# First attention and even mixer of a two-block model: stores on other queues, a modulation part moved, every fourth convolution tap on TensorE

## The chip, the cores and the metric

The kernel runs on one core of one Trainium2 chip. The metric is the device time of one execution in microseconds (us), lower is better.

## The reference

Two blocks run one after the other. The parts that this case is about, cut down:

```python
def first_block(x, c, ctx, c_ctx, ada_w, ...):
    for i in range(2):
        shift, scale, gate = split(silu(c) @ ada_w[i] + ada_b[i], 3)
        h_lat = rms_norm(x_lat, norm_w[i]) * (1 + scale) + shift       # 1024 tokens, width 1024
        ...                                                            # i == 0: also 256 context tokens
        y = attn_mixer(h_lat, h_ctx, ...) if i % 2 == 0 else hyena_mixer(h_lat, ...)
        x_lat = x_lat + gate * y
    return rms_norm(x_lat, final_norm_w)

def attn_project(h, ...):
    q_a, k_a, v_a, c_q, c_kv, k_pe, gate = split_cols(h @ w_in, ATTN_SPLITS)
    # 8 grouped heads of 64 on 2 key heads: q_a, k_a are normalised per head and rotated (rope)
    # 8 latent heads: q_m = norm(c_q) @ w_uq (64 + 32 rotated), k_m, v_m = norm(c_kv) @ w_ukv, k_pe shared
    ...
def mix(...):
    o = concat(softmax(q_a k_a) v_a, softmax(q_m k_m) v_m)             # keys: 256 context + 1024 tokens
    return (o * silu(gate)) @ w_out

def even_mixer(h, in_w, dw_w, dw_b, ...):                              # in second_block
    a_val, a_gate, q, k, v = split(h @ in_w, ...)
    u = causal_dwconv(a_val * sigmoid(a_gate), dw_w, dw_b)             # 512 channels, 31 taps each
    u = silu(layer_norm(u, ln_g, ln_b))
    o = stick_breaking_attention(rms_norm(heads(q)), rms_norm(heads(k)), heads(v))
    return concat(u, o) @ out_w
```

## The kernel before

Activations lie channels on partitions (128) and tokens along the free axis. Products at full precision are made from three matmuls: `split` (L100, L104) cuts an operand into a rounded high part (`...h`, ScalarE) and a rest (`...l`, VectorE), and `mm3` (L108 to L110) multiplies high by high, high by low and low by high. A framework of tiles and pools places the semaphores: a tile of a pool with n buffers waits until the one n tiles earlier is no longer read. It also sets each engine's order, from the order in which the code is written.

**A modulation row** is a product of a weight row block with the silu of `c`. `mods` (L226) loads 128x1024 weights at L228 on SyncE's queue and multiplies and sums them on VectorE at L236. It is a generator, one row block per `step`; `finish_aside` runs it to the end. Of the first block's 48 row blocks, 16 are needed before the first projection, and 32 (16 to 47) only later.

**First attention, projections** (`_a_project`, L338). `proj` (L348) multiplies the weights of one column block with 512 (or 256 context) tokens. Keys, then grouped queries, latent ranks and gates follow; each result goes through a norm per head (L405), `rope` (L388 to L395: a shuffle and three element-wise operations, one of them on GpSimd in 10 of 14 cases) and `store` (L411), which splits it into `sth` and `stl`, two buffers each, and writes the two to memory by SyncE's queue (L424). The destination holds two heads of 64 rows, so that its outermost size is 2 (4 for the rotated parts of latent queries). Values (`vstore`, L426) and gates (`gate`, L477, L480) are stored by the same queue, and weights (L328), rope tables and the 32 modulation blocks are loaded by it, the latter two buffers deep, one per projection. A second generator `both` makes the keys and values of the latent heads (22 steps) and their queries (12, L537); from the fifth projection on each loop turn takes one step of it. At the end `a_load` (L588) loads the first pair of heads on GpSimd's queue (qa, qb, ka, kb, v), and the steps left follow.

**First attention, attention** (`_a_attend`, L623). For 8 pairs of heads and 2 halves of the queries, 10 key blocks each: scores (L686), Exp on ScalarE (L123), the sum of weights on VectorE (`acc`, L735) and weighted values (L692). Meanwhile the next group's maximum is estimated: `guess` (L666) writes scores of 128 queries into `s`, a PSUM tile with a single buffer, and VectorE reduces it (L669). `finish` (L697 to L709) divides by the sum, with a tile `z`, one buffer. `moe_clear` (L1760) sets a tile of the same tag `z` to zero and stores it thirteen times to `m_y`, which the experts use much later; it is called in the second group.

**Even mixer** (`ev_mixer`, L1425). `conv(n)` runs four times on 128 channels: it makes value and gate by `proj_tile` (PSUM tag `pj`, three buffers), and `u` with 30 zeros ahead. Of the 31 taps the last starts `acc` on ScalarE, 20 of the rest go to VectorE (L1474, one fused multiply-add over 1024 tokens each), and every third to ScalarE, which multiplies (L1468), and GpSimd, which adds (L1470) into `accp`; L1476 adds the two sums. A generator again: `queries_keys` takes steps of it (its norm is L297 and L155 to L157), so that taps stand between the projections.

```python
                nc.vector.stream_shuffle(sh, x, mask)
                eng.tensor_tensor(out=x, in0=x, in1=ropes[0][:m, 0, t0:t0 + n], op=ALU.mult)
...
                if j % 3 == 2:
                    t = accp if first else cp.tile([P, T], F32, name="ct", tag="ct")
                    nc.scalar.mul(t, src, wcol)
```

Of the kernel before, what the change touches and what calls it, by code (L numbers as in the profile page):

```python
# [18 lines left out]
P = 128  # L19
# [69 lines left out]
class Kern:  # L89
# [175 lines left out]
    def phase_a(self, first, mod, M):  # L265

        tc = self.tc
        with tc.tile_pool(name="a_dram", bufs=1, space=DRAM) as dr:
# [5 lines left out]
            self._a_project(*first, S, mod)  # L274
            o_pool = tc.alloc_tile_pool(name="a_o", bufs=1, side="right")
            o = o_pool.tile([P, KT, T], F32, name="attn_o")
            self._a_attend(first[0], o, S, M)
# [60 lines left out]
    def _a_project(self, A, lat_ab, ctx_ab, S, mod):  # L338
        tc, nc, a = self.tc, self.nc, self.a
        PARTS = ((0, 512), (512, 512), (T, TC))  # L340
        if True:
# [6 lines left out]
            def proj(wc, c0, m, part, xh=hh, xl=hl, nk=KT):  # L348
                t0, n = part
                ps = pp.tile([P, 512], F32, name="mm", tag="mm")[:m, :n]  # L350
                if nk == KT:
                    self.step()
                for k in range(nk):
                    self.mm3(ps, wc[0][:, k, c0:c0 + m], wc[1][:, k, c0:c0 + m], xh[:, k, t0:t0 + n],
                             xl[:, k, t0:t0 + n], k == 0, k == nk - 1)
                return ps
# [21 lines left out]
            self.aside = self.mods(tp, a["ada_wT"].rearrange("l r d -> (l r) d"), ("c",), (mod,), 16, 48, 2)  # L378
# [9 lines left out]
            def rope(x, part, mask, eng=nc.gpsimd):  # L388
# [4 lines left out]
                eng.tensor_tensor(out=x, in0=x, in1=ropes[0][:m, 0, t0:t0 + n], op=ALU.mult)  # L393
# [17 lines left out]
            def store(x, dst, off, step, hs, d, pitch, part, rep=1):  # L411

                t0, n = part
                hl_ = [tp.tile([P, 512], F32R, name="st" + q, tag="st" + q)[:x.shape[0], :n] for q in "hl"]
                self.split(hl_[0], hl_[1], x)
                for i, t in enumerate(hl_):
# [7 lines left out]
                    nc.sync.dma_start(ap_of(dst, i * off * pitch + t0, dims), src.bitcast(F32))  # L424

            def vstore(ps, dst, b):  # L426
                t = tp.tile([P, 512], F32, name="vs", tag="vhl")[:, :ps.shape[1]]
                nc.scalar.copy(t, ps)
                nc.sync.dma_start(dst[:, b], t)
# [47 lines left out]
            def gate(m, pt, ps):  # L477
                g = work(P, 512)
                self.act(g, ps, AF.Silu)
                nc.sync.dma_start(S["gate"][m, :, pt[0]:pt[0] + 512], g)  # L480

            def key_rope(pt, ps):
# [4 lines left out]
                if pt[0] < T:  # L487
                    rope(kp, pt, swap8, nc.vector)
# [48 lines left out]
            def latent_queries():  # L537
                self.finish_aside()
                msc = 96.0 ** -0.5
                for m in range(6):  # L540
                    if m in (0, 4):
                        c = (0, 512) if m == 0 else (512, 256)
                        k = 2 * c[1]
                        w = A.wp.tile([P, 1024], F32, name="wraw", tag="wraw")[:, :k]
                        nc.sync.dma_start(w, a["w_uq"][:, 2 * c[0]:2 * c[0] + k])
                        wuq = [tp.tile([P, 1024], F32R, name="wq", tag="modw")[:, :k] for _ in "hl"]
                        self.split(*wuq, w)
                        wuq = [t.rearrange("p (k c) -> p k c", k=2) for t in wuq]
                    for pt in PARTS[:2]:
# [5 lines left out]
                        else:  # L555
                            rope(x, pt, swap8, nc.vector)
# [8 lines left out]
            for n, (ps, post) in enumerate(projections()):  # L565
# [3 lines left out]
                if n >= 4:  # L569
                    next(beside, None)  # L570
            last()
            self.finish_aside()
# [50 lines left out]
    def _a_attend(self, A, o, S, M):  # L623
# [7 lines left out]
        with tc.tile_pool(name="at_o", bufs=2) as op, tc.tile_pool(name="at_s", bufs=1, space=PSUM) as sp, \  # L631
                tc.tile_pool(name="at_t", bufs=3, space=PSUM) as tp, \
                tc.tile_pool(name="at_p", bufs=1, space=PSUM) as pp:
            st, gates = {}, {}

# [84 lines left out]
            for i, (hp, g) in enumerate(todo):  # L720
                if i == 1:
# [5 lines left out]
                for kb in range(NK):  # L727
# [23 lines left out]
            while pend:  # L751
                pend.pop(0)()
        for p in (A.ip[1], ptp, wp, A.ip[0]):
# [676 lines left out]
    def ev_mixer(self, F, x_pool, work, h, S):  # L1430
# [12 lines left out]
        def conv(n):  # L1443
# [17 lines left out]
            accp = cp.tile([P, T], F32, name="accp", tag="accp", bufs=1)  # L1461
            first = True
            for j in range(30):
                src = u[:, j:j + T]
                wcol = self.vec("ev_dw_w", j * 4 + n)
                if j % 3 == 2:
                    t = accp if first else cp.tile([P, T], F32, name="ct", tag="ct")
                    nc.scalar.mul(t, src, wcol)  # L1468
                    if not first:
                        nc.gpsimd.tensor_tensor(out=accp, in0=accp, in1=t, op=ALU.add)  # L1470
                    first = False
                    yield
                else:
                    nc.vector.scalar_tensor_tensor(out=acc, in0=src, scalar=wcol, in1=acc, op0=ALU.mult,  # L1474
                                                   op1=ALU.add)
            nc.gpsimd.tensor_tensor(out=acc, in0=acc, in1=accp, op=ALU.add)  # L1476
# [1080 lines left out]
```

## Time and profile before

| | |
|---|---|
| median of 3 runs | 4418.02 us (4414.76 to 4423.42) |
| the profiled execution's own time | 4418.37 us |
| its span, first to last instruction | 4416.6 us |
| mean granted TensorE clock | 0.91 of full speed |
| TensorE busy | 3641.1 us (82%) |
| VectorE busy | 2981.7 us (68%) |
| ScalarE busy | 1810.4 us (41%) |
| GpSimd busy | 1149.5 us (26%) |

In the profile PE is TensorE, PEld its weight loads, DVE VectorE, ACT ScalarE, POOL GpSimd and SP SyncE; a q behind the name is the engine's queue. L12 is line 12 of the kernel. An operation reads out<-in. The granted clock is TensorE's, as a share of full speed. DMA is the mean busy share of the core's 16 DMA engines. Shares over the whole span are averages over stages with different limits, so the stages are read one by one: the projections stand from 345 to 805 us, the attention from 822 to 1336, the convolutions of the even mixer from 2336 to 2590.

### The profile page before, as it was taken

Reading aid. Unit: us, or ns where it says so; the run is one execution under the profiler, and the core shown is the slowest. Engines: PE = TensorE matmul, PEld = TensorE weight load, DVE = VectorE, ACT = ScalarE, POOL = GpSimd, SP = SyncE. Lnnn points to the kernel's source line nnn. Section 1 sums busy time; section 2 is a strip of 40 time slices with the busy share of each in tenths; the row PEclk is TensorE's granted clock in tenths of the full one; section 3 lists DMA queues with packets and bytes.
Section 4 is the critical chain, followed back from the end, with each engine's and each line's share of the span. In section 5 each row is a group of like instructions: output and inputs, shape, how many; then the busy total and the mean of one; then the engine's idle time right before and its main releaser. Section 6 shows DMA issues by size and latency. Waiting matters only on the chain. (4 is left out here: it accounts for less than half of the span.)

```text
span 4416.6 us, 45389 instructions
## 1 busy us (share of the span) xinstructions
PE 3641.1 (82%) x16768; PEld 2823.9 (64%) x16768; DVE 2981.7 (68%) x3254; ACT 1810.4 (41%) x2470; POOL 1149.5 (26%) x640
## 2 busy tenths in 40 slices
PE   5786576599998999867787757788999788879997
PEld 4774454345556877756665646667888576767885
DVE  7995341577665676799678969755666576556664
ACT  4552231244443212111244435545556454436663
POOL 4630000011110001488304345331111133411112
PEclk9897788799999999988898879889999899989998
DMA  4553343422304786333321133227787511258876
GB/s 160 169 168 105 116 157 104 146 65 60 71 21 167 265 292 205 115 126 132 129 100 63 58 97 92 82 81 264 287 283 284 184 46 39 96 181 312 289 289 215
DMA packets 213107, 675.07 MB, mean 153 GB/s; under 512 B 40757, under 2 KB 66793, under 8 KB 177810
## 3 DMA queue, kind: packets, MB, share of 16 engines
q1 hardware_dynamic: 160738, 548.86, 35.7%
q0 software_dynamic: 44656, 97.06, 7.7%
q10 hardware_dynamic: 7488, 26.22, 1.5%
q8 instruction: 133, 2.18, 0.2%
q14 instruction: 92, 0.75, 0.1%
HBM read 538.04 MB, written 133.94 MB: 152 GB/s over the span
## 5 line engine op out<-in xcount | busy, mean ns | idle before, releaser
L104 DVE TENSOR_TENSOR wl<-wraw,wh 128x1024 fp32r<-128x1024 f32 (+1 forms) x212 | 330.0, 1565 | 223.1 <-ACT wh L100 206.9
L100 ACT CAST wh<-wraw 128x1024 fp32r<-128x1024 f32 (+1 forms) x212 | 276.0, 1312 | 448.8 <-DMA wraw<-in_ex_w_dram 151.1
L108 PE MATMUL pj<-hh,wh 128*128 128x512 f32 x1024 | 406.3, 397 | 19.4 <-ACT hh L881 7.6
L108 PE MATMUL mm<-hh,wh 128*128 128x512 f32 (+3 forms) x832 | 344.9, 415 | 82.6 <-ACT wh L100 22.3
L109 PE MATMUL pj<-hl,wh 128*128 128x512 f32 x1024 | 411.2, 402 | 0.0
L110 PE MATMUL pj<-hh,wl 128*128 128x512 f32 x1024 | 405.1, 396 | 0.7 <-DVE wl L104 0.7
L110 PE MATMUL mm<-hh,wl 128*128 128x512 f32 (+3 forms) x832 | 335.8, 405 | 7.4 <-DVE wl L104 7.3
L109 PE MATMUL mm<-hl,wh 128*128 128x512 f32 (+3 forms) x832 | 338.2, 406 | 1.0 <-POOL hl L104 0.8
L123 ACT ACTIVATE pt<-st 128x512 f32<-128x512 f32 x320 | 181.6, 598 | 225.0 <-PE st L686 211.0
L108 PEld LDWEIGHTS mm<-hh,wh 128*128 128x128 f32 (+1 forms) x832 | 165.5, 199 | 136.0 <-ACT wh L100 14.9
L669 DVE TENSOR_REDUCE mx<-s 128x1 f32<-128x1280 f32 x124 | 184.4, 1487 | 97.5 <-PE s L666 97.0
L236 DVE SCALAR_TENSOR_TENSOR modw<-modw,c 128x1024 f32<-128x1024 f32 x128 | 161.2, 1273 | 123.3 <-DMA modw<-in_ada_wT_dram 69.7
L108 PEld LDWEIGHTS pj<-hh,wh 128*128 128x128 f32 x1024 | 196.5, 192 | 67.1 <-ACT hh L881 10.0
L109 PEld LDWEIGHTS pj<-hl,wh 128*128 128x128 f32 x1024 | 196.8, 192 | 45.6 <-issue 4.3
L110 PEld LDWEIGHTS pj<-hh,wl 128*128 128x128 f32 x1024 | 196.2, 192 | 46.5 <-issue 4.3
L104 DVE TENSOR_TENSOR l<-raw,h 128x1024 fp32r<-128x1024 f32 x128 | 166.9, 1335 | 64.9 <-ACT h L100 62.7
L692 PE MATMUL ps_o<-pt,v 128*64 128x512 f32 x640 | 201.6, 609 | 0.0
L1326 PE MATMUL py<-c_g,ph 128*128 128x256 f32 x512 | 134.5, 423 | 79.6 <-DVE ph L1205 79.6
L110 PEld LDWEIGHTS mm<-hh,wl 128*128 128x128 f32 (+1 forms) x832 | 163.8, 197 | 47.7 <-DVE wl L104 10.2
L109 PEld LDWEIGHTS mm<-hl,wh 128*128 128x128 f32 (+1 forms) x832 | 165.1, 198 | 39.8 <-DVE hl L882 1.9
L2206 POOL DMA_INDIRECT xg<-m_h,idx x50 | 65.0, 1300 | 466.1 <-PE xt L2120 420.7
L735 DVE TENSOR_TENSOR acc<-acc,pt 128x1024 f32<-128x1024 f32 x128 | 158.8, 1241 | 21.1 <-ACT pt L123 18.4
(601 smaller groups left out, 9943.0 us busy)
## 6 DMA issues: line engine op xcount, KB each, us to landing
wraw<-in_ex_w_dram SPq DMA_DIRECT2D x128, 1024.0 KB
raw<-in_ex_w_dram SPq DMA_DIRECT2D x64, 1024.0 KB
modw<-in_mod_wT_dram SPq DMA_DIRECT2D x96, 512.0 KB
modw<-in_ada_wT_dram SPq DMA_DIRECT2D x48, 512.0 KB
m_y<-ys ACTq DMA_DIRECT2D x48, 512.0 KB
ks<-kt SPq DMA_DIRECT2D x64, 256.0 KB
wraw<-in_w_hy_in_dram SPq DMA_DIRECT2D x16, 1024.0 KB
kk<-ks SPq DMA_DIRECT2D x28, 512.0 KB
```

Of the source, the lines that this page charges most:

```text
L100: nc.scalar.copy(hi, src)
L104: e.tensor_tensor(out=lo, in0=src, in1=hi.bitcast(F32), op=ALU.subtract)
L108: nc.tensor.matmul(ps, wh, xh, start=first, stop=False)
L109: nc.tensor.matmul(ps, wh, xl, start=False, stop=False)
L110: nc.tensor.matmul(ps, wl, xh, start=False, stop=last)
L123: ins = act.activation(out, in_, func, **kw).ins
L236: nc.vector.scalar_tensor_tensor(out=junk, in0=w, scalar=1.0, in1=c, op0=ALU.mult, op1=ALU.mult, accum_out=o[:, j:j + 1])
L669: nc.vector.tensor_reduce(out=mx[:, j:j + 1], in_=s[:, :TK] if own else m3, op=ALU.max, axis=AX.X, negate=True)
L692: nc.tensor.matmul(ps_o[e * 64:(e + 1) * 64], st[2 * hp + e]["v"][:, kb], pt[:, e], start=kb == 0, stop=kb == NK - 1)
L735: nc.vector.tensor_tensor(out=acc, in0=acc, in1=pt, op=ALU.add)
L1326: nc.tensor.matmul(py[:, j], d["ph"][:, r, cs], g[:, m, r], start=k == 0, stop=k == 3)
L2206: self.nc.gpsimd.indirect_dma_start(out=out, out_offset=None, in_=src, in_offset=bass.IndirectOffsetOnAxis(ap=ix, axis=0))
```

## The change

Stores of `_a_project`: four buffers instead of two for `sth`, `stl` and the values; high parts, values and gates go out on ScalarE's queue, low parts on GpSimd's. SyncE's queue keeps the loads. `rope` multiplies on VectorE in all cases. The 32 modulation blocks leave `_a_project`; `_a_attend` makes them, in a pool with two buffers, one after the third and one after the seventh key block of each group from the second on, the rest at the end. The second generator starts with the eleventh projection instead of the fifth, so six of its steps are left for the time of the first pair's loads; its weights come by the same buffers as the others. `moe_clear` is called in the fourth group instead of the second. In the even mixer taps 3, 7, ... 27 (seven of 30) become matmuls: ScalarE multiplies the identity with the tap's column (`dg`, 128x128), TensorE multiplies `dg` with the shifted `u` at full precision into `side`, a PSUM tile of tag `pj`, and VectorE adds `side` at the end; the other 23 taps are VectorE's.

```diff
@@ _a_project(self, A, lat_ab, ctx_ab, S): without mod
             def proj(wc, c0, m, part, xh=hh, xl=hl, nk=KT):
...
-                if nk == KT:
-                    self.step()
...
-            self.aside = self.mods(tp, a["ada_wT"].rearrange("l r d -> (l r) d"), ("c",), (mod,), 16, 48, 2)
...
-            def rope(x, part, mask, eng=nc.gpsimd):
+            def rope(x, part, mask):
...
-                eng.tensor_tensor(out=x, in0=x, in1=ropes[0][:m, 0, t0:t0 + n], op=ALU.mult)
+                nc.vector.tensor_tensor(out=x, in0=x, in1=ropes[0][:m, 0, t0:t0 + n], op=ALU.mult)
@@ store, vstore, gate
-                hl_ = [tp.tile([P, 512], F32R, name="st" + q, tag="st" + q)[:x.shape[0], :n] for q in "hl"]
+                hl_ = [tp.tile([P, 512], F32R, name="st" + q, tag="st" + q, bufs=4)[:x.shape[0], :n] for q in "hl"]
...
-                    nc.sync.dma_start(ap_of(dst, i * off * pitch + t0, dims), src.bitcast(F32))
+                    (nc.gpsimd if i else nc.scalar).dma_start(ap_of(dst, i * off * pitch + t0, dims), src.bitcast(F32))
...
-                t = tp.tile([P, 512], F32, name="vs", tag="vhl")[:, :ps.shape[1]]
+                t = tp.tile([P, 512], F32, name="vs", tag="vhl", bufs=4)[:, :ps.shape[1]]
                 nc.scalar.copy(t, ps)
-                nc.sync.dma_start(dst[:, b], t)
+                nc.scalar.dma_start(dst[:, b], t)
...
-                nc.sync.dma_start(S["gate"][m, :, pt[0]:pt[0] + 512], g)
+                nc.scalar.dma_start(S["gate"][m, :, pt[0]:pt[0] + 512], g)
@@ latent_queries and the loop
-                self.finish_aside()
...
-                        w = A.wp.tile([P, 1024], F32, name="wraw", tag="wraw")[:, :k]
-                        nc.sync.dma_start(w, a["w_uq"][:, 2 * c[0]:2 * c[0] + k])
-                        wuq = [tp.tile([P, 1024], F32R, name="wq", tag="modw")[:, :k] for _ in "hl"]
-                        self.split(*wuq, w)
-                        wuq = [t.rearrange("p (k c) -> p k c", k=2) for t in wuq]
+                        wuq = self.a_wload(A, a["w_uq"][:, 2 * c[0]:2 * c[0] + k], 2, c[1])
...
-                if n >= 4:
+                if n >= 10:
                     next(beside, None)
             last()
-            self.finish_aside()
@@ _a_attend(self, A, o, S, M, mod)
+            self.aside = self.mods(op, self.a["ada_wT"].rearrange("l r d -> (l r) d"), ("c",), (mod,), 16, 48, 2)
...
-                if i == 1:
+                if i == 3:
                     self.moe_clear(op, M)
...
                         pend.append(functools.partial(finish, hp, g, ps_o, acc))
+                    if i and kb % 4 == 2:
+                        self.step()
...
+            self.finish_aside()
@@ ev_mixer, conv
-            accp = cp.tile([P, T], F32, name="accp", tag="accp", bufs=1)
-            first = True
+
+            side = F.pp.tile([P, T], F32, name="side", tag="pj")
             for j in range(30):
-                src = u[:, j:j + T]
                 wcol = self.vec("ev_dw_w", j * 4 + n)
-                if j % 3 == 2:
-                    t = accp if first else cp.tile([P, T], F32, name="ct", tag="ct")
-                    nc.scalar.mul(t, src, wcol)
-                    if not first:
-                        nc.gpsimd.tensor_tensor(out=accp, in0=accp, in1=t, op=ALU.add)
-                    first = False
+                if j % 4 == 3:
+                    dg = cp.tile([P, P], F32, name="dg", tag="dg", bufs=3)
+                    nc.scalar.mul(dg, self.ident, wcol)
+                    for t in (0, 512):
+                        nc.tensor.matmul(side[:, t:t + 512], dg, u[:, j + t:j + t + 512], start=j == 3, stop=j == 27)
                     yield
                 else:
...
-            nc.gpsimd.tensor_tensor(out=acc, in0=acc, in1=accp, op=ALU.add)
+            nc.vector.tensor_tensor(out=acc, in0=acc, in1=side, op=ALU.add)
```

SyncE's queue in the projections, near the first key stores. Before (`modw` is a modulation block, `wraw` weights, `s_k` and `s_km` the keys):

```order
L228 DMA modw<-in_ada_wT_dram 128x1024 x5
L328 DMA wraw<-in_w_attn_in_dram 128x1024
L424 DMA s_k<-sth 2x64x512
L424 DMA s_km<-sth 2x64x512
L228 DMA modw<-in_ada_wT_dram 128x1024
L424 DMA s_k<-stl 2x64x512
L424 DMA s_km<-stl 2x64x512
```

The same queue now, from the first rope table to the end of the projections and beyond:

```order
L381 DMA ropes<-in_ropes_dram 128x2048
L512 DMA wraw<-in_w_ukv_dram 128x512
L328 DMA wraw<-in_w_attn_in_dram 128x1024 x6
L512 DMA wraw<-in_w_ukv_dram 128x512
L328 DMA wraw<-in_w_attn_in_dram 128x1024 x3
L328 DMA wraw<-in_w_attn_in_dram 128x256
```

Stores and modulation blocks are gone from between the weights. ScalarE in the middle of the projections now (`wk` is a gate or query in work, `mm` a projection's PSUM tile, `s_q` the queries):

```order
L477 DMA s_gate<-wk 128x512
L100 CAST sth<-wk 128x512
L100 CAST sth<-mm 128x512
L421 DMA s_q<-sth 2x64x512
L421 DMA s_km<-sth 2x64x512
L100 CAST sth<-mm 128x512
L287 ACTIVATE sqa<-mm 128x512
```

Each store stands in ScalarE's own order, between its casts and activations. VectorE in the attention, second group, now (`mx` is the guess, `m_l_129` the sums of the modulation):

```order
L661 TENSOR_REDUCE mx<-s 128x1
L236 SCALAR_TENSOR_TENSOR modw,m_l_129<-modw,c 128x1024
L661 TENSOR_REDUCE mx<-s 128x1
L699 SCALAR_TENSOR_TENSOR z<-sm,y 128x512
L727 TENSOR_TENSOR acc<-acc,pt 128x1024
```

Before, a guess and a sum took turns there, and nothing else stood between them but the two operations of `finish`. TensorE in a convolution of the even mixer now (`pj` is a projection, `blk_70` the norm's block matrix):

```order
L108 MATMUL pj<-hh,wh 128x512
L109 MATMUL pj<-hl,wh 128x512
L110 MATMUL pj<-hh,wl 128x512
L1464 MATMUL side<-u,dg 128x512 x4
L297 MATMUL mm<-sqa,blk_70 128x512
L1464 MATMUL side<-u,dg 128x512 x4
L108 MATMUL pj<-hh,wh 128x512
```

Before, the projection's matmuls ran on from one side of L297 to the other, with nothing but it between them.

## Rows read from the trace of the kernel before

**Rows 1.** Stretches by engine; columns: from:to, length, busy time of each engine, clock, DMA share, GB/s

```profile
core 0: us, PE busy (x) PEld busy (x) DVE busy (x) ACT busy (x) POOL busy (x), PEclk, DMA share, GB/s
345.00:805.00 460.00, 262.35 (x999) 194.11 (x997) 164.56 (x268) 115.02 (x182) 21.69 (x17) 0.77 0.37 118
...
822.00:1336.00 514.00, 502.76 (x1982) 264.80 (x1980) 366.34 (x300) 227.28 (x399) 78.60 (x61) 0.99 0.27 71
2336.00:2407.00 71.00, 56.11 (x219) 43.01 (x218) 60.56 (x44) 28.75 (x33) 30.42 (x10) 0.88 0.17 63
2407.00:2473.00 66.00, 47.07 (x177) 35.53 (x176) 60.55 (x44) 29.21 (x33) 30.68 (x10) 0.82 0.21 75
2473.00:2539.00 66.00, 52.01 (x228) 40.85 (x227) 60.87 (x44) 29.77 (x34) 30.71 (x10) 0.87 0.12 45
2539.00:2590.00 51.00, 35.99 (x261) 34.76 (x259) 47.14 (x34) 15.61 (x23) 33.17 (x12) 0.90 0.21 63
```

**Rows 2.** Timeline of SyncE's queue, projections; columns: start, us, instruction

```profile
376.52 0.50 SPq L424 DMA_DIRECT2D s_k<-stl  x1
377.12 5.48 SPq L424 DMA_DIRECT2D s_km<-stl  x1
...
411.86 2.63 SPq L424 DMA_DIRECT2D s_k<-stl  x1
```

**Rows 3.** Stretches, while only key stores are under way

```profile
383.00:402.00 19.00, 6.86 (x20) 5.02 (x21) 4.06 (x7) 1.93 (x3) 0.00 (x0) 0.56 0.13 51
```

**Rows 4.** DMA issues, 345 to 822 us; count, KB each, us to landing

```profile
modw<-in_ada_wT_dram SPq DMA_DIRECT2D x31, 512.0 KB
...
s_qm<-sth SPq DMA_DIRECT2D x12, 256.0 KB
...
s_km<-sth SPq DMA_DIRECT2D x9, 256.0 KB
...
s_q<-sth SPq DMA_DIRECT2D x8, 256.0 KB
...
ka<-s_k POOLq DMA_DIRECT2D x1, 640.0 KB, 26.4
```

**Rows 5.** Waits, 345 to 822 us: total, times, longest

```profile
DVE stl L104 <- DMA s_qm<-stl: 39.6, 5, 11.5
...
PE mm L297 <- ACT sqa L287: 32.7, 6, 11.5
...
PE mm L108 <- ACT wq L100: 18.4, 1, 18.4
...
PE mm L297 <- DVE sqa L291: 14.6, 1, 14.6
```

**Rows 6.** Stretches, while three loads of GpSimd's queue are under way

```profile
2622.00:2626.00 4.00, 0.00 (x0) 0.00 (x0) 0.00 (x0) 0.00 (x0) 0.00 (x0) 0.50 0.43 156
```

**Rows 7.** Modulation's group by line; wait for the scores; ScalarE's timeline; a stretch

```profile
L236 DVE SCALAR_TENSOR_TENSOR modw<-modw,c 128x1024 f32<-128x1024 f32 x32 | 40.0, 1251 | 69.7 <-DMA modw<-in_ada_wT_dram 69.7
...
DVE mx L669 <- PE s L666: 94.3, 58, 4.7
...
866.55 0.60 ACT L123 ACTIVATE z<-sm 128x512 f32<-128x512 f32 x1 [9.55 <-DMA m_y<-z]
...
862.00:866.00 4.00, 0.00 (x0) 0.00 (x0) 0.00 (x0) 0.00 (x0) 0.00 (x0) 0.73 0.12 50
```

**Rows 8.** Even mixer: taps by line and by duration; TensorE's timeline; a wait

```profile
L1474 DVE SCALAR_TENSOR_TENSOR o<-u,vecs,o 128x1024 f32<-128x1024 f32 x80 | 165.0, 2063 | 6.4 <-ACT o L1458 5.2
...
L1474 DVE SCALAR_TENSOR_TENSOR o<-u,vecs,o x80: 1268/1284/3355, 2336.3 to 2583.6; 128x1024 f32<-128x1024 f32 x80
...
2455.89 0.39 PE L108 MATMUL pj<-hh,wh 128*128 128x512 f32 x1
2456.12 1.02 PE L297 MATMUL mm<-sqa,blk 128*128 128x512 f32 x2
...
2457.21 0.39 PE L110 MATMUL pj<-hh,wl 128*128 128x512 f32 x1
...
PE mm L297 <- DVE o L1474: 28.8, 3, 9.9
```

More of the change, by code (lines that the diff above doesn't have):

```diff
@@ L273, in phase_a @@
             S["gate"] = dr.tile([KT, P, T], F32, name="s_gate")
-            self._a_project(*first, S, mod)
+            self._a_project(*first, S)
             o_pool = tc.alloc_tile_pool(name="a_o", bufs=1, side="right")
             o = o_pool.tile([P, KT, T], F32, name="attn_o")
-            self._a_attend(first[0], o, S, M)
+            self._a_attend(first[0], o, S, M, mod)
         return o, o_pool
@@ L336, in a_wchunk, with _a_project @@
         return self.a_wload(A, self.a["w_attn_in"][:, A.off - KT * c:A.off], KT, c)
-    def _a_project(self, A, lat_ab, ctx_ab, S, mod):
+    def _a_project(self, A, lat_ab, ctx_ab, S):
         tc, nc, a = self.tc, self.nc, self.a
@@ L487, in key_rope @@
                 if pt[0] < T:
-                    rope(kp, pt, swap8, nc.vector)
+                    rope(kp, pt, swap8)
                 store(kp, S["km"][0, 64:], 96, 193, 1, 32, TK, pt, rep=8)
@@ L555, in latent_queries @@
                         else:
-                            rope(x, pt, swap8, nc.vector)
+                            rope(x, pt, swap8)
                             store(x, S["qm"][4 * (m - 4), 0, 64:], 96, 192, 4, 32, T, pt)
@@ L621, in a_load, with _a_attend @@
         return qa, qb, ka, kb, v
-    def _a_attend(self, A, o, S, M):
+    def _a_attend(self, A, o, S, M, mod):
         tc, nc = self.tc, self.nc
@@ L1460, in conv @@
             yield
-            accp = cp.tile([P, T], F32, name="accp", tag="accp", bufs=1)
-            first = True
+            side = F.pp.tile([P, T], F32, name="side", tag="pj")
             for j in range(30):
-                src = u[:, j:j + T]
                 wcol = self.vec("ev_dw_w", j * 4 + n)
-                if j % 3 == 2:
-                    t = accp if first else cp.tile([P, T], F32, name="ct", tag="ct")
-                    nc.scalar.mul(t, src, wcol)
-                    if not first:
-                        nc.gpsimd.tensor_tensor(out=accp, in0=accp, in1=t, op=ALU.add)
-                    first = False
+                if j % 4 == 3:
[3 more added lines that the diff above has]
+                        nc.tensor.matmul(side[:, t:t + 512], dg, u[:, j + t:j + t + 512], start=j == 3, stop=j == 27)
                     yield
                 else:
-                    nc.vector.scalar_tensor_tensor(out=acc, in0=src, scalar=wcol, in1=acc, op0=ALU.mult,
+                    nc.vector.scalar_tensor_tensor(out=acc, in0=u[:, j:j + T], scalar=wcol, in1=acc, op0=ALU.mult,
                                                    op1=ALU.add)
-            nc.gpsimd.tensor_tensor(out=acc, in0=acc, in1=accp, op=ALU.add)
+            nc.vector.tensor_tensor(out=acc, in0=acc, in1=side, op=ALU.add)
         def queries_keys(n, beside):
```

## The prediction

> **What bounds the kernel now.** I read the stretches by engine first [rows 1]. In each stage the reader is to see which engine, if any, is busy nearly all the time. In the first attention's attention loop TensorE is busy 502.76 of 514 us at a granted clock of 0.99: TensorE bounds it. In the projections that precede it (460 us) no engine does: TensorE 262.35, VectorE 164.56, ScalarE 115.02, and the clock is 0.77. Something that is no engine sets that stage. In the four convolution cycles of the even mixer (71, 66, 66 and 51 us) VectorE is the fullest, with 60.56, 60.55, 60.87 and 47.14.
>
> Then I read SyncE's queue in the projections [rows 2]. The issue of a 256 KB store of keys takes 0.50 us when nothing stands ahead of it, and holds SyncE for 5.48 us when something does; one half as large holds it for 2.63. While only such stores are under way the DMA share is 0.13 and 51 GB/s [rows 3]: 0.13 of 16 engines is two engines. The destination of these stores has an outermost size of 2 (two heads), and 256 KB at 51 GB/s are 5.1 us, which is the time of the issue. So SyncE's one queue passes these stores through two of 16 engines, one after another, and every load stands behind them.
>
> The table of DMA issues [rows 4] says how many there are. Two-head stores of 256 KB for hi: 8 of the 9 of s_km, 8 of s_q, 8 of the 12 of s_qm and, by the code, 2 of s_k, so 26 x 5.1 = 133 us. Nine smaller ones (by the code the 256-column parts, one of s_k and four of s_km, and the four of s_qm that have 4 as outermost size) are 9 x 2.6 = 23. That is 156 us for hi, and as much for lo: 312. The 31 modulation loads take 2.6 each if their 512 KB run at some 200 GB/s (an estimate from the 0.37 share and the 118 GB/s of the stage, doubled as the loads use more engines), 80 us. That leaves 68 for weights, gates and values, and the sum is the stage. The waits agree [rows 5]: VectorE's split waits 39.6 us for the buffer of a store of latent queries alone.
>
> **The change, part by part.**
>
> *Stores off SyncE's queue, four buffers, modulation gone from the stage.* SyncE keeps weight and rope loads, so nothing is queued behind a store there. Hi stores, values and gates go out on ScalarE's queue (38 hi, 20 values, 16 gates: 74 issues by 0.50 us [rows 2], 37 us, so ScalarE has 115 + 37 = 152 us of work), lo stores on GpSimd's, which has nothing else there but the loads of the first pair's operands at the end. The hi stores still want two engines for 156 us. Whether lo takes two other engines the trace has no row for in this stage; the nearest is a stretch later on where only three loads of GpSimd's queue with an outermost size of 2 are under way: a share of 0.43, so 6.9 engines [rows 6]. Three transfers on one pair would show 0.13. I take it that lo goes beside hi. The Trainium skill says so too (DMA: Bandwidth & Descriptors, "Why a DMA increments its semaphore by 16 and not by 1"): a hardware queue takes the lowest-numbered engines that the outermost sizes allow, GpSimd's takes as many consecutive ones from a moving start; 0.13 and 0.43 agree with it.
>
> What is left is TensorE. Its 262.35 us at a clock of 0.77 are 202 us at full clock. At a clock of about 0.9 the 202 are 225. The waits of TensorE that are no store's I keep: norms 32.7 and 14.6, the second weight 18.4 [rows 5], together 65.7. The loads of the first pair land 28 us after the last store that they need (26.4 for keys [rows 4], plus its landing); six latent-query projections stay beside them. So 225 + 66 + 28 = 319 instead of 460: **-141**. ScalarE's 152 and the hi stores' 156 are under it. The ends: at today's clock with 45 us at the end as now, 262 + 66 + 45 = 373, **-87**; with TensorE at full clock and the waits down by a third, 202 + 44 + 26 = 272, **-188**. The multiply of the rope on VectorE (10 more, 7 us) and the missing 40 of the modulation are off the path.
>
> *Modulation in the attention.* VectorE gets 32 x 1251 ns = 40 us [rows 7] on 366.34 of 514. It has 148 idle, 94.3 of them waiting for TensorE's scores `s` [rows 7], so it is ahead of TensorE for the most part. But the scores have one buffer: a step that falls just before the maximum of `s` keeps TensorE's next guess waiting for up to 1.25 us. Between 0 and 40 I take **+8**, a fifth: near the lower end, since TensorE's idle is 11 of 514 with VectorE at 71%. The loads are 32 x 512 KB on SyncE, idle there at a DMA share of 0.27.
>
> *Clearing of the expert buffer two groups later.* ScalarE waited 9.55 us for m_y's stores to leave tile z [rows 7], and TensorE behind it (busy 0.00 from 862 to 866, clock 0.73). There z is stored thirteen times while the first group's end wants it. Two groups later the same tile is wanted at the same distance, but the loads of the start are over; SyncE's queue also holds modulation loads then. I take **-8**; nothing if the wait only moves.
>
> *Even mixer.* VectorE: 80 taps take 165.0 us, a mean of 2063 ns, while the shortest takes 1268 and the median 1284 [rows 8]: the long ones stand beside GpSimd's adds. Now GpSimd is empty there, and 92 taps by 1.28 and four final adds of some 1.3 are 123: 42 less. TensorE gets 7 x 2 x 4 = 56 full-precision matmuls of 128x512. The price: from the norm's matmul at 2456.12 to the next but one at 2457.21 are 1.09 us, less 0.23 for the one between (as from 2455.89 to 2456.12), 0.86 [rows 8]; 56 x 0.86 = 48 us. TensorE's work at full clock is busy time by clock over the four cycles [rows 1], 49.4 + 38.6 + 45.2 + 32.4 = 166, and 214 with the new. VectorE is left with 229 - 42 = 187. So the bound passes from VectorE to TensorE: 254 now, 214 if TensorE never waited. It waits, since `side` keeps one of three projection buffers for the whole convolution, so the next chunk's second projection starts only after the final add; today's waits of TensorE for taps are 28.8 [rows 8]. I take half of it over the 214: 229, **-25**. The ends: -40, and +48 if all the matmuls stand in the open.
>
> Sum: -141 + 8 - 8 - 25 = -166 on the profiled execution's 4418.37, so **4252 us**. Its own time lies 0.35 over the median of the runs, so the median is predicted by the same number.
>
> **The rivals.**
>
> *The stores meet again.* Both queues use the same two engines, or ScalarE, held at its issues as SyncE was, works no faster. Then 312 us of stores stand one after another, 40 us to the first and 28 after the last: 380, -80, in all 4418 - 80 - 25 = 4313. For it: a store with two heads holds its issuer 5 us [rows 2], and ScalarE has work of its own behind. Against: the share of 0.43 [rows 6], and 152 + 156 is still less than 319. A rule of the Trainium skill speaks for it (DMA: Bandwidth & Descriptors, "Issuing engines are not separate DMA queues"): DMAs run on the same 16 engines whoever starts them, and another issuer saves the issuing time alone. By it the time is this rival's. Chance 0.2.
>
> *The even mixer pays.* TensorE waits for each 128x128 diagonal from ScalarE and for `side`: the 48 us stand in the open. 4418 - 141 + 48 = 4325. Against: two projections' worth of matmuls are queued between taps. Chance 0.12.
>
> *Slower: TensorE's clock in the attention.* The steps inserted on VectorE break TensorE's row of work, and the granted clock of 0.99 falls, as it does where TensorE stood still at 862 to 866 (0.73) [rows 7]. The gain of 166 is gone when the 514 us become 680, at a clock of 0.99 x 514 / 680 = 0.75; at 0.7 they are 727, and the time is 4252 + 213 = 4465. Against: one step stands for 1.25 us, ScalarE's wait there was 9.55, and the mean of the stage is 0.99 with it in. Chance 0.04.
>
> The change may also leave the stage as it is, since what I call SyncE's bound were the chains of norm and rope themselves: about 4400, 0.02.
>
> **How the numbers follow.** The forecast has 0.62 and gives the time; with its own ends it reaches from 4180 to 4340. To leave out no more than 2 in 10 the range takes in the first two rivals: 4175 to 4345. A measurement of this kernel can tell about 0.2% from no change. Faster by more: forecast, the first two rivals and most of the last, 0.94; same 0.02; slower 0.04.
>
> **What would show it.** In the profile after: first score matmul at 650 to 680 us instead of 805, no modulation row before it; SyncE's issues there short; ScalarE's issue rows at most 3 us; attention 505 to 530 us at a clock over 0.95; no 9 us wait for m_y; taps at 1.28 us, and cycles near 57 us with TensorE the fullest. I am wrong if ScalarE's store issues take 5 us each (first rival), if `side` matmuls are waited for (second), or if the attention's clock is under 0.9 (third).

## The result, and the profile after

The changed kernel takes 4248.85 us (median of 4 runs, 4247.26 to 4254.81) against 4416.39 for the kernel before: a ratio of 0.9624, with a 95% interval of 0.961 to 0.9638. The profiled execution's own time is 4247.26 us, its span 4245.5, the mean granted clock 0.931. The forecast was 4252 us.

The first view is again that of the stretches, for the changed kernel, in the columns of [rows 1]: the projections, the attention, the convolutions of the even mixer.

```profile
345.00:638.00 293.00, 239.31 (x1002) 181.63 (x1000) 128.74 (x203) 112.28 (x179) 32.07 (x42) 0.90 0.46 128
...
659.00:1197.00 538.00, 516.45 (x1987) 263.51 (x1985) 401.50 (x371) 230.06 (x402) 76.84 (x61) 0.98 0.38 101
2200.00:2266.00 66.00, 64.55 (x252) 47.02 (x251) 52.92 (x53) 22.56 (x31) 0.00 (x0) 1.00 0.26 91
2266.00:2326.00 60.00, 59.89 (x232) 43.17 (x231) 48.29 (x50) 21.20 (x29) 0.00 (x0) 1.00 0.20 73
2326.00:2386.00 60.00, 59.87 (x255) 42.99 (x254) 48.38 (x50) 22.58 (x33) 0.00 (x0) 1.00 0.12 45
2386.00:2414.00 28.00, 28.00 (x185) 23.18 (x184) 27.54 (x28) 3.42 (x9) 0.29 (x1) 1.00 0.19 57
```

The reader is to see three things. The projections are 293 us long instead of 460, with the clock at 0.90 instead of 0.77. The attention got longer, 538 instead of 514, with 35 us more of VectorE. In the even mixer GpSimd's column is empty, and TensorE is busy all the time at full clock.

For stage by stage arithmetic I take four marks that every kernel here has: the first matmul of the guessed scores, the first cast of the attention's output, the first `u` of the convolutions and the first sum over their result. They come from the view of one tile's instructions (first and last start, us). Before:

```profile
L666 PE MATMUL s<-ka,qa x372: 276/393/796, 805.2 to 1298.5; 96*128 96x512 f32 x64, 128*128 128x512 f32 x60, 96*128 96x256 f32 x32, 128*128 128x256 f32 x30
...
L100 ACT CAST hh<-attn_o x16: 610/614/617, 1336.7 to 1348.1; 128x512 fp32r<-128x512 f32 x16
...
L1456 DVE TENSOR_TENSOR u<-pj,sg x4: 1216/1222/1228, 2333.8 to 2536.7; 128x1024 f32<-128x1024 f32 x4
...
L1551 POOL TENSOR_TENSOR s<-o x2: 1707/1736/1765, 2587.5 to 2589.2; 128x512 f32<-128x512 f32 x2
```

Changed:

```profile
L658 PE MATMUL s<-ka,qa x372: 276/393/796, 638.4 to 1158.8; 96*128 96x512 f32 x64, 128*128 128x512 f32 x60, 96*128 96x256 f32 x32, 128*128 128x256 f32 x30
...
L100 ACT CAST hh<-attn_o x16: 609/614/617, 1197.0 to 1208.4; 128x512 fp32r<-128x512 f32 x16
...
L1451 DVE TENSOR_TENSOR u<-pj,sg x4: 1217/1226/1226, 2200.2 to 2378.8; 128x1024 f32<-128x1024 f32 x4
...
L1544 POOL TENSOR_TENSOR s<-o x2: 1299/1536/1774, 2413.7 to 2415.0; 128x512 f32<-128x512 f32 x2
```

| stretch | before | changed | difference | forecast |
|---|---|---|---|---|
| to the first score matmul | 805.2 | 638.4 | -166.8 | -141 |
| attention, to the first cast | 531.5 | 558.6 | +27.1 | 0 |
| to the first `u` | 997.1 | 1003.2 | +6.1 | |
| convolutions, to the first sum | 253.7 | 213.5 | -40.2 | -25 |
| to the end of the span | 1829.1 | 1831.8 | +2.7 | |
| span | 4416.6 | 4245.5 | -171.1 | -166 |

That the sum met the forecast within 5 us is luck: errors of -25.8, +27.1 and -15.2 leave -13.9, and the two stretches without a forecast, whose code nobody touched, bring back 8.8. These two differ by a few us from kernel to kernel (993 to 1003, and 1829 to 1846 in the kernels below); I have no reading of that.

The kernels below were timed once each, except the last. Five kernels with the same projections (the changed one, e_mod_bufs4, e_clear1, e_tap5, e_tap_dve) have the first score matmul at 637.6 to 643.7 us, and three with the same attention as well (the changed one, e_tap5, e_tap_dve) take 558.6 to 563.5 us for it. Differences of 5 or 6 us in these stretches are not read as effects.

### The profile page after: what moved, and what is told of

It reads as the page before. It is cut to its first block, busy times and chain, and to the rows that moved or that the text cites. A ratio compares the mean times of both kernels' runs of the same rounds, so it can differ in the third digit from the quotient of the medians.

```text
span 4245.5 us, 45506 instructions
## 1 busy us (share of the span) xinstructions
PE 3659.2 (86%) x16880; PEld 2817.5 (66%) x16880; DVE 2932.2 (69%) x3280; ACT 1777.8 (42%) x2458; POOL 1031.8 (24%) x628
## 5 line engine op out<-in xcount | busy, mean ns | idle before, releaser
L108 PE MATMUL mm<-hh,wh 128*128 128x512 f32 (+3 forms) x832 | 338.0, 407 | 37.6 <-ACT wh L100 19.4
L1321 PEld LDWEIGHTS py<-c_g,ph 128*128 128x128 f32 x512 | 107.4, 215 | 102.5 <-issue 67.2
```

The lines of the kernel that those rows point to most:

```text
L108: nc.tensor.matmul(ps, wh, xh, start=first, stop=False)
L1321: nc.tensor.matmul(py[:, j], d["ph"][:, r, cs], g[:, m, r], start=k == 0, stop=k == 3)
```

## Experiments: what set the projections

**Stores back on SyncE's queue**, modulation still in the attention, four buffers kept:

```diff
-                    (nc.gpsimd if i else nc.scalar).dma_start(ap_of(dst, ...), src.bitcast(F32))
+                    nc.sync.dma_start(ap_of(dst, ...), src.bitcast(F32))
-                nc.scalar.dma_start(dst[:, b], t)            # values; gates likewise
+                nc.sync.dma_start(dst[:, b], t)
```

> The changed kernel with all stores of the projections back on SyncE's queue; modulation stays in the attention. Theory (two-head stores pass one queue through two DMA engines one after another): 312 us of stores plus some 68 of weights, gates and values, so the first score matmul near 725 us (700 to 745; 638 in the changed kernel, 805 before), SyncE held about 5 us per two-head store, whole time near 4335. Rival (it was the 31 modulation loads and their sums on VectorE that made the stage long): first score matmul below 665, whole time near 4270.

Measured: 4350.6 us, first score matmul at 735.4. So of the 166.8 us the other queues give 97, and the rest of the change (no modulation in the stage, four buffers, the later second generator, the rope on VectorE) 70. The forecast had put 80 for the modulation loads' time in the queue. This run does not split the 70, and further down two buffers, or the earlier start of the second generator, cost over 30 us each. The queues alone do not make the whole gain.

**Low parts on SyncE's queue**, high parts on ScalarE's:

```diff
-                    (nc.gpsimd if i else nc.scalar).dma_start(ap_of(dst, ...), src.bitcast(F32))
+                    (nc.sync if i else nc.scalar).dma_start(ap_of(dst, ...), src.bitcast(F32))
```

> The changed kernel with low parts on SyncE's queue instead of GpSimd's, high parts still on ScalarE's. Theory (two hardware queues take the same lowest two engines, GpSimd's does not): 312 us of stores on two engines again, first score matmul at 695 to 730 us, whole time 4305 to 4340, issues held on both queues. Rival (each queue has a pair of its own, a second queue of any kind is enough): first score matmul at 635 to 655 us, whole time near 4250.

Measured: 4344.29 us, first score matmul at 738.2, no sooner than with one queue. The timelines of SyncE's and ScalarE's queues in this kernel (start, us) and the stretch in which both are held:

```profile
415.12 19.01 SPq L421 DMA_DIRECT2D s_km<-stl  x2
```

```profile
416.80 5.94 ACTq L421 DMA_DIRECT2D s_km<-sth  x1
423.45 9.53 ACTq L421 DMA_DIRECT2D s_km<-sth  x1
```

```profile
416.00:433.00 17.00, 11.53 (x40) 8.25 (x39) 0.69 (x1) 1.08 (x2) 0.00 (x0) 0.80 0.13 50
```

Two queues store at the same time, and the DMA share is 0.13 at 50 GB/s: what one queue shows alone [rows 3]. The view of this stretch by queue gives each of them half of it (packets, MB, share of 16 engines; q1 is SyncE's, q10 ScalarE's, and the view calls both hardware queues, while GpSimd's, q0, is a software queue):

```profile
q1 hardware_dynamic: 214, 0.43, 6.6%
q10 hardware_dynamic: 213, 0.43, 6.6%
```

So the two hardware queues use the same two engines for these stores. In the changed kernel the low parts are GpSimd's, and a stretch with both under way reads otherwise, as a whole and by queue:

```profile
455.00:465.00 10.00, 3.96 (x11) 2.65 (x12) 0.69 (x1) 1.08 (x2) 1.56 (x2) 0.66 0.37 76
```

```profile
q0 software_dynamic: 1161, 0.42, 26.1%
q10 hardware_dynamic: 171, 0.34, 10.7%
```

0.37 of 16 are six engines: about two for ScalarE's stores and four for the two low parts that are under way on GpSimd's queue. So the first rival's condition is real, but it is met by another queue pair than the change uses. The Trainium skill (DMA: Bandwidth & Descriptors, "Why a DMA increments its semaphore by 16 and not by 1") has it so: the lowest-numbered engines for a hardware queue, a moving start for GpSimd's. Both stretches agree. What the Trainium skill says of another issuer, that it saves the issuing time alone (DMA: Bandwidth & Descriptors, "Issuing engines are not separate DMA queues"), holds for the 738.2 and not for the 638.4.

**One head per store**, all on SyncE's queue:

```diff
                     elif hs > 1:
-                        dims = [[step * pitch, hs]] + dims
-                    (nc.gpsimd if i else nc.scalar).dma_start(ap_of(dst, i * off * pitch + t0, dims), src.bitcast(F32))
+                        for q in range(hs):
+                            nc.sync.dma_start(ap_of(dst, (i * off + q * step) * pitch + t0, dims),
+                                              src[q * d:(q + 1) * d].bitcast(F32))
+                        continue
+                    nc.sync.dma_start(ap_of(dst, i * off * pitch + t0, dims), src.bitcast(F32))
```

> All stores on SyncE's queue as in e_all_sp, but each two-head store cut into two stores of one head (64 rows, so an outermost size of 64). Theory (the outermost size of 2 sets two engines): the cut stores spread, none holds SyncE for 5 us, and the first score matmul comes at 640 to 660 us although nothing left SyncE's queue. Rival (one queue is the limit, whatever the shape): it stays where e_all_sp has it, or later by the 52 more issues of about 0.5 us.

Measured: 4205.19 us, first score matmul at 604.1, better than expected and 34 us sooner than in the changed kernel, with every store on one queue. Its SyncE timeline (x2: the two heads):

```profile
412.33 1.19 SPq L421 DMA_DIRECT2D s_km<-sth  x2
413.61 1.19 SPq L421 DMA_DIRECT2D s_km<-stl  x2
414.89 1.19 SPq L421 DMA_DIRECT2D s_km<-sth  x2
416.18 1.19 SPq L421 DMA_DIRECT2D s_km<-stl  x2
417.46 0.54 SPq L328 DMA_DIRECT2D wraw<-in_w_attn_in_dram  x1
```

Eight half-sized stores, the data of four uncut ones, and a weight load are issued in 6 us; uncut, one store held the queue 5.48 [rows 2]. The shape was the bound, and another queue is the weaker cure.

**Two store buffers:**

```diff
-                hl_ = [tp.tile([P, 512], F32R, name="st" + q, tag="st" + q, bufs=4)[:x.shape[0], :n] for q in "hl"]
+                hl_ = [tp.tile([P, 512], F32R, name="st" + q, tag="st" + q)[:x.shape[0], :n] for q in "hl"]
-                t = tp.tile([P, 512], F32, name="vs", tag="vhl", bufs=4)[:, :ps.shape[1]]
+                t = tp.tile([P, 512], F32, name="vs", tag="vhl")[:, :ps.shape[1]]
```

> The changed kernel with two store buffers instead of four. Theory (queues, not buffers): ScalarE's and VectorE's splits wait a little more for stores, the first score matmul comes 5 to 15 us later than 638. Rival (the four buffers carry a good part of the gain): it comes 40 us or more later.

Measured: 4285.39 us, first score matmul at 670.8, 32 later: between the two, nearer to the rival. While the high parts still go through two engines, a deeper store ring is worth a fifth of the gain. The forecast had given the buffers no term of their own.

**The second generator from the fifth projection:**

```diff
-                if n >= 10:
+                if n >= 4:
```

> The changed kernel with the second generator starting at the fifth projection as before. Theory (the later start leaves six latent-query projections for the time of the first pair's loads, in which TensorE is idle): all 34 steps now lie before those loads, the first score matmul comes 10 to 20 us later than 638. Rival (the start only spreads the stores): within 5 us of 638, or earlier.

Measured: 4277.78 us, first score matmul at 674.8, 36 later. The side is the theory's, the size twice what it allowed. TensorE's idle time in the trace shows two parts. After 606 us it is 43.7 us, against 22.7 in the changed kernel, which fits the theory. From 345 to 410 us it is 26.6 against 4.9, which does not: there the second generator's key stores now meet the first key stores, and ScalarE stands at an issue. (Between 410 and 606 it is 19.4 against 26.1.) The first stretch, and the longest issue in it:

```profile
345.00:410.00 65.00, 38.38 (x167) 27.74 (x166) 33.41 (x55) 21.39 (x39) 5.68 (x7) 0.84 0.28 77
```

```profile
374.57 13.70 ACTq L421 DMA_DIRECT2D s_km<-sth  x1
```

## Experiments: the attention

**Without the modulation blocks:**

```diff
-            self.aside = self.mods(op, self.a["ada_wT"].rearrange("l r d -> (l r) d"), ("c",), (mod,), 16, 48, 2)
+            nc.vector.memset(mod[:, 16:48], 0.0)
```

(and without the steps that call it, so that the 32 blocks are left out)

> The changed kernel without the 32 modulation blocks 16 to 47: their loads and sums are left out (zeros in their place). From the first score matmul to the first cast of the attention's output the kernel before takes 531.5 us, the changed one 558.6. Theory (the 32 steps on VectorE, in order with the maxima of the single score buffer, made the attention longer): it falls to 518 to 532 us, and TensorE's wait for the maximum goes. Rival (the move of the clearing, or the low-part stores still going out at the start): it stays above 545.

Measured: 4227.6 us; the stretch falls to 529.5. The steps make the stretch 29 us longer, three quarters of the 40 us that VectorE spends on them, where the forecast said a fifth.

**Four buffers for a block:**

```diff
-            self.aside = self.mods(op, ..., ("c",), (mod,), 16, 48, 2)
+            self.aside = self.mods(op, ..., ("c",), (mod,), 16, 48, 4)
```

> The changed kernel with four instead of two buffers for a modulation block in the attention. Theory (about half of the loss is VectorE standing at a step whose load is late, 22.1 us in 5 waits, with the maximum behind it): the same stretch falls from 558.6 to 540 to 550 us and VectorE's waits for modulation loads are under 5. Rival (every step costs by its own length and place): 554 us or more.

Measured: 4226.04 us; the stretch is 539.6, so 19 of the 29 us are gone. The waits in the changed kernel (in all, times, longest):

```profile
DVE modw L236 <- DMA modw<-in_ada_wT_dram: 22.1, 5, 10.7
...
PE s L658 <- DVE mx L661: 16.2, 6, 8.9
```

and with four buffers, where VectorE waits for no modulation load any more:

```profile
PE s L658 <- DVE mx L661: 0.3, 1, 0.3
```

How that chain works is in the changed kernel's timeline of VectorE:

```profile
1050.74 1.22 DVE L236 SCALAR_TENSOR_TENSOR modw<-modw,c 128x1024 f32<-128x1024 f32 x1
...
1054.29 1.22 DVE L236 SCALAR_TENSOR_TENSOR modw<-modw,c 128x1024 f32<-128x1024 f32 x1
...
1056.84 1.22 DVE L236 SCALAR_TENSOR_TENSOR modw<-modw,c 128x1024 f32<-128x1024 f32 x1
...
1068.72 1.23 DVE L236 SCALAR_TENSOR_TENSOR modw<-modw,c 128x1024 f32<-128x1024 f32 x1 [10.66 <-DMA modw<-in_ada_wT_dram]
```

Four steps stand within a few us in VectorE's order, while two buffers hold two loads ahead. The fourth waits 10.66 us for a load that runs beside the next pair's operands, and the maximum of the scores stands behind it in order: TensorE's 8.9 us wait. The 32 steps are written two per group, but the scheduler that sets the order placed them in bunches.

**The clearing back in the second group:**

```diff
-                if i == 3:
+                if i == 1:
                     self.moe_clear(op, M)
```

> The changed kernel with the clearing of the expert buffer back in the second group. Theory (its move saved ScalarE's 9.55 us wait for tile z): that wait is back and the stretch grows from 558.6 by 5 to 12 us. Rival (the wait only moved, or modulation loads fill the queue ahead of it): within 3 us of 558.6.

Measured: 4260.7 us; the stretch is 568.1, longer by 9.5, and the wait is back:

```profile
704.66 0.60 ACT L123 ACTIVATE z<-sm 128x512 f32<-128x512 f32 x1 [8.07 <-DMA m_y<-z]
```

That step of the forecast (-8) held.

## Experiments: the even mixer

**Five taps on TensorE:**

```diff
-                if j % 4 == 3:
+                if j % 6 == 5:
-                        nc.tensor.matmul(side[...], dg, u[...], start=j == 3, stop=j == 27)
+                        nc.tensor.matmul(side[...], dg, u[...], start=j == 5, stop=j == 29)
```

> The changed kernel with five of the 30 taps (every sixth) on TensorE instead of seven. Theory (TensorE, busy all the time at a clock of 1.00, bounds the convolutions now): from the first u to the first square sum after them the changed kernel takes 213.5 us (253.7 before); 16 matmuls by 0.86 us fewer bring it to 198 to 206. Rival (VectorE with its 92 taps bounds it): 8 more taps by 1.28 us make it 218 to 226.

Measured: 4265.93 us; the stretch is 230.0. Theory and rival both miss. A wait is there that the changed kernel does not have:

```profile
PE pj L108 <- DVE o L1469: 9.7, 2, 4.8
```

L1469 is the final add of `side`. TensorE's next projection waits for the PSUM buffer that `side` keeps; these 9.7 us are part of the 16.5 that the stretch is longer. With five yields instead of seven the taps are also spread otherwise between the projections, so this run decides between neither.

**All taps on VectorE:**

```diff
-                if j % 4 == 3:
-                    dg = cp.tile([P, P], F32, name="dg", tag="dg", bufs=3)
-                    nc.scalar.mul(dg, self.ident, wcol)
-                    for t in (0, 512):
-                        nc.tensor.matmul(side[:, t:t + 512], dg, u[:, j + t:j + t + 512], start=j == 3, stop=j == 27)
-                    yield
-                else:
-                    nc.vector.scalar_tensor_tensor(...)
-            nc.vector.tensor_tensor(out=acc, in0=acc, in1=side, op=ALU.add)
+                nc.vector.scalar_tensor_tensor(...)
+                if j % 4 == 3:
+                    yield
```

> The changed kernel with all 30 taps of the even mixer on VectorE and none on TensorE, ScalarE or GpSimd. Theory (GpSimd's adds slowed VectorE's taps from 1.28 to 2.06 us): 120 taps take 154 us, less than the 165 of the 80 before, and the stretch of 253.7 before becomes 225 to 245, so the old helpers made it no shorter. Rival (taps of this kind take 2 us beside anything else): 120 taps take 240 us and the stretch 310 or more.

Measured: 4249.51 us, the changed kernel's time, and a stretch of 213.2, the changed kernel's 213.5. The taps of this kernel by line:

```profile
L1459 DVE SCALAR_TENSOR_TENSOR o<-u,vecs,o 128x1024 f32<-128x1024 f32 x120 | 153.2, 1278 | 2.3 <-ACT o L1453 1.3
```

120 taps alone take 153.2 us, where 80 beside GpSimd took 165.0 [rows 8]. This run takes ScalarE's multiplications away as well as GpSimd's adds; the trace of the kernel before tells the two apart. Of its 80 taps, the 47 that a GpSimd add overlaps by less than 0.5 us take 1.27 to 1.29 us, eight of them beside one of ScalarE's multiplications. The other 33 take 2.58 to 3.36 us, five of them with no such multiplication beside them. Two taps that follow one another, and the row of three GpSimd adds that stands beside the first:

```profile
2364.86 3.35 DVE L1474 SCALAR_TENSOR_TENSOR o<-u,vecs,o 128x1024 f32<-128x1024 f32 x1
...
2368.74 1.27 DVE L1474 SCALAR_TENSOR_TENSOR o<-u,vecs,o 128x1024 f32<-128x1024 f32 x1
```

```profile
2357.84 9.30 POOL L1470 TENSOR_TENSOR accp<-accp,ct 128x1024 f32<-128x1024 f32 x3
```

So the 40 us came from taking GpSimd's adds away. The matmuls that replaced them brought nothing that VectorE would not have done in the same time. The stretch as a whole, in the changed kernel and in this one:

```profile
2200.00:2414.00 214.00, 212.31 (x917) 156.36 (x916) 177.13 (x178) 69.75 (x102) 0.29 (x1) 1.00 0.20 69
```

```profile
2204.00:2417.00 213.00, 191.53 (x962) 159.84 (x960) 207.14 (x210) 61.82 (x84) 1.44 (x2) 0.94 0.23 79
```

In the one TensorE is busy nearly all the time, in the other VectorE; that the two bounds come out equal is chance.

## A version that beats both

**One-head stores on SyncE's queue, two store buffers, modulation in the projections** as in the kernel before; the later second generator, the rope, the clearing and the even mixer as changed. The modulation's part of the edit (the attention loses its steps; the stores are cut as above):

```diff
-            self._a_project(*first, S)
+            self._a_project(*first, S, mod)
...
                 ps = pp.tile([P, 512], F32, name="mm", tag="mm")[:m, :n]
+                if nk == KT:
+                    self.step()
...
+            self.aside = self.mods(tp, a["ada_wT"].rearrange("l r d -> (l r) d"), ("c",), (mod,), 16, 48, 2)
...
             last()
+            self.finish_aside()
```

> One-head stores on SyncE's queue, two store buffers, and the modulation back in the projections: of the changed kernel's first part only the start of the second generator, the rope and the clearing stay. Theory (the shape of the stores was the bound; with it gone the modulation's loads fit beside): first score matmul at 615 to 645 us, the attention stretch 518 to 532, whole time 4185 to 4215. Rival (the modulation's 31 loads and 40 us of VectorE bind the stage themselves): first score matmul later than 665.

Measured: 4185.71 us; first score matmul at 613.2, the attention stretch 524.4. Its stretch of the projections:

```profile
345.00:585.00 240.00, 221.29 (x939) 168.69 (x939) 153.91 (x254) 109.18 (x169) 0.00 (x0) 0.95 0.70 199
```

All loads and stores are back on one queue, which now moves 199 GB/s at a share of 0.70, and TensorE has 221.29 of 240 at a clock of 0.95; another 28 us, with the loads of the first pair, follow to the first score matmul. The modulation costs 9 us here (613.2 against 604.1, with two buffers instead of four as well) and 29 in the attention.

The same kernel once more, in four runs:

> The kernel of e_head_modproj again, timed in rounds: one-head stores on SyncE's queue, two store buffers, modulation in the projections, all else as changed. Theory (the shape of the stores was the bound of the projections and the modulation does not belong into the attention): 4180 to 4195 us, a ratio to the kernel before of 0.946 to 0.950, below the changed kernel's 0.9624 by more than both intervals. Rival (the one look was a lucky run): 4220 or more.

Measured: 4185.71 us (4 runs, 4184.37 to 4186.81), a ratio to the kernel before of 0.9472, interval 0.9456 to 0.9489: below the changed kernel's whole interval.

## Why the prediction was right

**The bound of the projections** was named rightly: two-head stores, two engines, one queue. Both ways of taking it away show it (e_head_sp by the shape, the change by the queue), and e_lo_sp shows that a second queue on the same two engines does not help. That low parts go beside high ones was taken from one stretch of another stage [rows 6]; it held. The prediction's sum of the stage could not fail, since its 68 us for weights, gates and values were what was left over; e_all_sp is its test, 390 us from 345 to 735.4 where 312 + 68 = 380 were reckoned.

**Its size** was 26 us too small. TensorE's busy time came to 239.31 at 0.90, 215 at full clock, near the 202 that the sum rests on. The mis-sized terms are the waits kept at 66 and the loads at the end at 28, 94 together: TensorE is idle 293 - 239 = 54 us, 23 of them after 606 us and 31 before. The first, middle and last of the stretches are

```profile
345.00:410.00 65.00, 60.15 (x278) 47.10 (x277) 43.24 (x70) 33.08 (x61) 4.11 (x5) 0.97 0.32 88
...
410.00:506.00 96.00, 69.96 (x260) 51.37 (x258) 38.48 (x60) 33.06 (x46) 11.90 (x15) 0.85 0.35 100
...
606.00:638.00 32.00, 9.30 (x41) 7.33 (x40) 9.32 (x18) 7.47 (x13) 7.89 (x11) 0.68 0.69 186
```

TensorE waits hardly at all at the start, where I had kept the norm waits as no store's. The other queues are not enough for that: with the same queues and the earlier second generator (e_n4) TensorE has 38.38 us there, and with every store on SyncE's queue and the later one (e_all_sp) 55.54. The later start, to which the forecast gave no term of its own, leaves two of the second generator's key stores on ScalarE's queue in this time instead of four, the first at 398 us instead of 370.

**ScalarE's issues** were said to stay at 3 us or less, 74 of them by 0.50, 37 us. The count is right; added up from the timeline they take 113 us. Seven are longer than 3 us between 415 and 505, 46.9 us in all, and three more after 600, one of them 10.22. The longest of the seven:

```profile
460.51 9.41 ACTq L421 DMA_DIRECT2D s_km<-sth  x1
```

So the sign of the first rival, issues of 5 us, came for seven of the 74, and a part of that rival was there (ScalarE held as SyncE was). From 410 to 506, where most of these issues stand, TensorE is idle 26 us in the changed kernel. In e_head_sp it is not idle there at all:

```profile
410.00:506.00 96.00, 96.00 (x407) 75.34 (x406) 58.78 (x90) 53.06 (x73) 0.00 (x0) 1.00 0.66 170
...
345.00:604.00 259.00, 228.28 (x996) 176.54 (x995) 126.85 (x201) 113.01 (x180) 4.79 (x7) 0.94 0.55 146
```

Of the 34 us by which e_head_sp is ahead, 23 are idle time of TensorE (54 against 31) and 11 busy time, at a clock of 0.94 instead of 0.90. That is the price of the two-head stores that the changed kernel keeps; how much of it is ScalarE standing still, no run separates.

**The modulation in the attention** was the step that failed: +8 forecast, 29 measured. I took a fifth of 40 since VectorE is idle for 148 us. The idle time is of no use where the order is fixed: a step that waits for its load keeps the maximum behind it waiting. I had called SyncE's queue idle and never asked whether two buffers carry a load past the pair's operands. Nineteen of the 29 us are that. What the other ten are is not shown: with four buffers TensorE's waits for the maximum are down to 0.3 us. TensorE's clock held: 0.98 over the stage, so the third rival's mechanism (0.75) did not come; but in the worst 50 us, with the 8.9 us wait, it fell:

```profile
1050.00:1100.00 50.00, 41.07 (x163) 22.43 (x161) 29.97 (x30) 16.75 (x29) 8.32 (x7) 0.90 0.51 111
```

**The clearing** gave 9.5 where 8 were forecast. With the modulation's 29 that makes +19.6 for the attention, and measured were +27.1. The 7.5 us left over stay open. About four of them are in the first 20 us after the first score matmul, before and changed:

```profile
805.20:825.20 20.00, 13.80 (x47) 8.48 (x47) 16.30 (x25) 4.01 (x6) 1.05 (x2) 0.73 0.28 86
```

```profile
638.40:658.40 20.00, 11.72 (x29) 7.06 (x29) 15.32 (x24) 2.21 (x4) 2.07 (x3) 0.50 0.41 117
```

Busy time by clock is 10.1 us of work there before, and 5.9 now.

**The even mixer** came out at the lower end of its range, -40.2 for -25: TensorE waits for nothing there, and 213.5 us are the 214 of work at full clock that the text had worked out. The half of today's waits that I added was not owed. But the reason was half right only. VectorE's taps did fall to 1.28 us, all of them, and that is the gain (e_tap_dve); that TensorE should take seven was not needed for it.

## What to carry to other kernels

Before moving a transfer to another queue, read the DMA share of a stretch in which it runs alone: 0.13 of 16 says that its shape uses two engines, and here cutting it so that its outermost size is 64 instead of 2 cured that on the queue where it was. A helper engine that slows the engine it helps (1.28 to 2.06 us per tap in the mean) is to be counted with that price; try the helped engine alone first. Work put on an engine with idle time costs its wait and not its length when it waits for a load in front of something that the bounding engine needs: give it buffers before giving it a place.

## What the runs showed that was not expected

Two hardware queues that store at the same time in the two-head shape move together what one moves alone: 50 GB/s at a share of 0.13 in e_lo_sp, and a first score matmul at 738.2 us against 735.4 with one queue. And a kernel with every tap on VectorE, in which TensorE and GpSimd do nothing for the convolution, is as fast as one that gives seven of 30 to TensorE: 213.2 against 213.5 us. And one setting of the order of the code, the turn at which the second generator starts, is worth 36 us of the changed kernel's gain (674.8 against 638.4), about as much as the two-head shape still costs it.
